# Layer 0's opening in two halves of the rows, with its modulation as dot products along the free axis and five latent blocks feature by feature

## The chip, the cores and the metric

The kernel runs on one core of a Trainium2 chip. The metric is the device time of one execution in microseconds (us), with the median of several runs. The engines are TensorE (PE), VectorE (DVE), ScalarE (ACT) and GpSimd (POOL); SP issues nearly all of the DMAs, in the order of its own queue.

## The reference, cut to what matters

A transformer of two layers over 1024 tokens of 1024 features, batch 1, float32. Each layer normalises its rows, modulates them by a vector computed from `c`, and projects them. Layer 0 has eight latent (MLA) heads and eight stick-breaking heads, layer 1 differential heads.

```python
c_act = jax.nn.silu(c)
for i in range(DEPTH):
    mod = c_act @ ada_w[i] + ada_b[i]
    shift, scale, gate = jnp.split(mod, 3, axis=-1)
    h = rms_norm(x, norm_g[i]) * (1.0 + scale[:, None, :]) + shift[:, None, :]
    ...
proj = h @ w_in
cuts = np.cumsum([MLA_Q_LORA, MLA_KV_LORA, MLA_ROPE, SB_W, SB_W, SB_W]).tolist()
cq, ckv, kr, q_sb, k_sb, v_sb, z = jnp.split(proj, cuts, axis=-1)
q = (rms_norm(cq, q_norm_g) @ w_uq).reshape(B, S, MLA_HEADS, MLA_NOPE + MLA_ROPE)
kv = (rms_norm(ckv, kv_norm_g) @ w_ukv).reshape(B, S, MLA_HEADS, MLA_NOPE + MLA_V)
```

`cq` has 384 columns and `ckv` 256: five blocks of 128 columns, called the latent blocks here (numbers 16 to 20 of the weights).

## The kernel before, in words

Float32 products run on TensorE as three passes over parts rounded to 12 bits: `split` (L155) takes hi on ScalarE (L159) and lo = src - hi on VectorE or GpSimd (L154), and `mm3` (L172) is hi x hi, hi x lo, lo x hi. `wprep` (L164) loads the weights of a block of 128 columns (512 KB) into `w_st`, a staging tile of a pool with two buffers, and splits them. The features of the normalised rows lie on the partitions: `hT[k]` holds features 128 k and on of all 1024 tokens, hi and lo.

The opening (L500 to L706) works under one pool, `a0`. All eight tiles of x are loaded and their squares summed, on ScalarE (L526) and VectorE (L523) in turn; `rstd_cols` (L188) makes 1/rms by thirteen small VectorE instructions; the rows are scaled in place (L532, L534). `ada_block(k)` (L538) then computes shift and scale of 128 features: `ada_st`, 1 MB of weights with the input feature on the partitions, is multiplied by `c_act` and accumulated by eight VectorE instructions of 128x256 (L542, L544) into `ack`, whose partitions TensorE sums with a matrix of ones (L547); four transposes of each half of the tokens follow (L554), and `modulate` (L237) scales and shifts them on ScalarE into `hf` and splits them, the lo part on GpSimd for blocks 1 to 6.

The first three latent blocks run feature by feature: while block k of `hT` is made, the 18 matmuls of block k - 1 run into six PSUM banks. Blocks 19 and 20 follow one after the other through `latent` (L611) and `dense_fm` (L177). The latents' evacuations store hi and lo parts to DRAM; `behind` is the last store of the first three. The modulation of layer 1 and both gates come from `ada_rest` (L589): two sets n = 0, 1 of eight loads of 1 MB each and 64 VectorE sweeps of 128x512 (L478, L480) into `acc`, and column sums of `acc` on TensorE (L487). It is a generator, stepped by `more(n)`, and every step is placed after `ready` (the last block of `hT`) and `behind`. Then come the rotated shared key `krt` (L642, 48 matmuls), the row factors `te` and `to` (L681 to L686), and four z blocks (L700), each two halves of 24 matmuls through a bank of a pool of three (`s_bank`), evacuated by ScalarE (L249) and a VectorE product (L251). The first head's projection, `qk_dense` into banks called `psd`, opens the attention.

The order within each engine is set when the kernel is built: a scheduler lays the instructions of the program out engine by engine and interleaves what is written in sequence, `tc.issue_after(x)` holds what is written inside it behind x, and a tile of a pool waits for the last reader of the buffer that it takes over.

Of the kernel before, what the change touches and what calls it, by code (L numbers as in the profile page):

```python
# [72 lines left out]
def kernel(ctx, tc, a, out):  # L73
# [33 lines left out]
    # scratch in DRAM  # L107
# [19 lines left out]
    # constants  # L127
# [49 lines left out]
    def dense_fm(w, rhs, evac, bank=None):  # L177
        """feature-major rows of one block of 128 columns, in two halves of the tokens"""
# [9 lines left out]
    def rstd_cols(pool, ss, n, scale, eps, name, extra=None, bufs=2):  # L188
        """(scale * ss + eps * extra) ** -0.5 of [P, n] columns"""
# [16 lines left out]
    def row_out(pool, cols, n, dst, bank):  # L206
        """[P, n] columns (query in block, block) to rows of n blocks in DRAM"""
# [22 lines left out]
    def row_sums(tile_of, nt, bank):  # L230
        """sums over the partitions of tile_of(t), as columns [P, nt]"""
# [14 lines left out]
    def z_evac(z, func, scale):  # L246
        """z * sigmoid(z), or twice that from tanh(z / 2)"""
# [16 lines left out]
    def v_rows(vs, hi, lo, n):  # L264
        """token-major halves of the values in vs; hi(g), lo(g) of four token tiles"""
# [13 lines left out]
    def pieces(i):  # L279
        """(first key, keys, computed keys) of the banks of query block i"""  # L280
# [5 lines left out]
    def scores(i, pairs, mask):  # L286
        """pairs of (stationary, moving) summed into the scores of query block i, one bank a piece"""
# [12 lines left out]
    def transpose_chunk(c, pa, pb):  # L300
        """[q, k] weights of query blocks 2c, 2c+1 to tiles [k, (kb 2j+1 | kb 2j), 256 q]"""
# [18 lines left out]
    def pv_chunk(dst, tiles, passes):  # L320
        """dst[dv, 256] = sum over key blocks; passes(kb) -> [(stationary, 0 hi | 1 lo)]"""
# [39 lines left out]
    def qk_dense(w, hT, b_t, bank=None):  # L361
        """[qh;qh], [ql;0], [kh;kl] of one head whose weights are [q | k]"""
# [21 lines left out]
    def par_view(ap, par, seq=False):  # L384
        """the tokens of chunks par and 2 + par; with seq of chunks 2 par and 2 par + 1"""
# [26 lines left out]
    def finish_half(pool, pv, par, e, ot, seq=False):  # L412
        """add the two halves ([vh|vl] or [vl|vh]) of a bank holding the chunks of par_view"""
# [7 lines left out]
    def load_wo(layer, half, f2s, alloc, gate, eng):  # L421
        """feature blocks 2 f2, 2 f2 + 1 of one half of the columns, times the gate, split"""
# [34 lines left out]
    def out_half(ys, wo, fs, x_, xr, bank):  # L457
        """x_ = xr + rows of y times columns of wo"""
# [11 lines left out]
    def ada_sweep(pool, src, acc):  # L470
        """acc[p, n] = sum over kk of c[128 kk + p] ada_w[128 kk + p, n] for 2048 columns"""
# [11 lines left out]
    def ada_cols(dst, bias, acc):  # L483
        """sums over the partitions of the 2048 columns of acc, as [P, 16], and the bias"""
# [9 lines left out]
    X_TAGS = [("lsq0", 1), ("lsq1", 1), ("lsq2", 1), ("zb", 2), ("zb", 2), ("lat_h", 2), ("lat_h", 2), ("lat_l", 2)]  # L494

    # =====================================================================
    # layer 0: modulation, transposed rows, latents
    # =====================================================================
    hT = [(res(f"h0h{k}"), res(f"h0l{k}")) for k in range(KC)]
    with tc.tile_pool(name="a0", bufs=1, reuse_waits="tile") as a0:  # L500
        sgc = a0.tile([P, 8], F32, name="sgc")
        nc.scalar.activation(sgc, c_sb, AF.Sigmoid)
        nc.vector.tensor_mul(c_act, c_sb, sgc)
        ada_st = {}

        def ada_load(k):
            ada_st[k] = a0.tile([P, KC, 256], F32, name="ada_st", tag="ld", bufs=NLD)
            dma(ada_st[k].rearrange("p r c -> p (r c)"), a["ada_k"][k])
            return ada_st[k]

        # normalised rows
        xts = []
        junka = a0.tile([P, 2, D], F32, name="junka", tag="acc")
        for g in range(2):
            ss = a0.tile([P, 4], F32, name="ss", tag="ss", bufs=2)
            for j in range(4):
                t = 4 * g + j
                tag, bufs = X_TAGS[t]
                xt = a0.tile([P, D], F32, name="xt", tag=tag, bufs=bufs)
                dma(xt, a["x"][t * P:t * P + P, :])  # L520
                if j % 2:
                    junk = a0.tile([P, D], F32, name="junk", tag="junk")
                    nc.vector.tensor_tensor_reduce(junk, xt, xt, op0=ALU.mult, op1=ALU.add, scale=1.0, scalar=0.0,  # L523
                                                   accum_out=ss[:, j:j + 1])
                else:
                    nc.scalar.activation(junka[:, 0, :], xt, AF.Square, accum_out=ss[:, j:j + 1])  # L526
                xts.append(xt)
            rs = rstd_cols(a0, ss, 4, 1.0 / D, 1e-6, "rc")
            for j in range(4):
                xt = xts[4 * g + j]  # L530
                if SC[4 * g + j] == "a":
                    nc.scalar.activation(xt, xt, AF.Copy, scale=rs[:, j:j + 1])  # L532
                else:
                    nc.vector.tensor_scalar(xt, xt, rs[:, j:j + 1], None, op0=ALU.mult)  # L534
            if g == 0:
                ada_load(0)

        def ada_block(k):  # L538
            """modulation of features 128 k and on, applied to their transposed rows"""
            st = ada_st[k] if k in ada_st else ada_load(k)  # L540
# [7 lines left out]
            nc.vector.tensor_tensor(modc[0][:, k::8], ps[:, 0:2], adab[:, k:16:8], op=ALU.add)  # L548
            nc.vector.scalar_tensor_tensor(gsc[0][:, k:k + 1], modc[0][:, 8 + k:9 + k], 1.0, ng[:, k:k + 1],
                                           op0=ALU.add, op1=ALU.mult)  # L550
            for g in range(2):
                tr = t_bank()
                for j in range(4):
# [654 lines left out]
```

## Time and profile before

| | |
|---|---|
| runs | 1490.88, 1488.34, 1491.48 us, median 1490.88 |
| profiled execution: span on the profile | 1489.6 us |
| TensorE busy | 1394.9 us, 94% |
| VectorE busy | 956.8 us, 64% |
| ScalarE busy | 670.5 us, 45% |
| GpSimd busy | 446.2 us, 30% |
| DMA | 189.85 MB, mean 127 GB/s |

The page's busy times are unions over the whole span, so they hide in which stretch an engine is waited for. The timeline lists instructions of one engine by their start, merged where they follow each other in one form, with the idle time just before them and what ended it. The granted clock is TensorE's, 1.00 for the full 2.4 GHz.

### The profile page before, as it was taken

The page shows a single profiled execution, that of the slowest core. Times are in us where ns is not written, and L with a number is a line of the kernel's source. Part 1 is how long each engine was busy: PE and PEld are TensorE (multiplying, and loading weights), DVE is VectorE, ACT ScalarE, POOL GpSimd, SP SyncE. Part 2 cuts the span into 40 slices and gives each one's busy share as a digit, 9 for nine tenths or more (in the row PEclk, how much of TensorE's full clock was granted, in tenths as well). Part 3 has the DMA queues.
Part 4 walks back from the last instruction along what each step waited for, and adds up shares of the span by engine and source line. Part 5 has one row for each costly group of instructions (what it writes and reads, how often), then busy time and mean ns, then how long its engine had stood idle before and what let it go on. Part 6 is the DMA issues. An engine that isn't in the chain of part 4 may idle for free.

```text
span 1489.6 us, 20993 instructions
## 1 busy us (share of the span) xinstructions
PE 1394.9 (94%) x7328; PEld 1160.7 (78%) x7328; DVE 956.8 (64%) x2155; ACT 670.5 (45%) x1368; POOL 446.2 (30%) x509
## 2 busy tenths in 40 slices
PE   3899999999998899999879899999999999997797
PEld 2777888888886688887767688888888888886686
DVE  7769637667779865576557526665565756567674
ACT  4452145555556653555345324444444535354321
POOL 1534221132427354635133321133121222134100
PEclk9999999999999999999989999999999999999899
DMA  9269522131224166433747131324232324346262
GB/s 375 67 261 382 206 77 75 49 90 50 75 69 186 36 188 213 136 123 100 215 136 268 29 108 48 86 85 114 71 100 64 92 64 114 78 111 179 82 201 93
DMA packets 109640, 189.85 MB, mean 127 GB/s; under 512 B 8736, under 2 KB 70040, under 8 KB 107488
## 3 DMA queue, kind: packets, MB, share of 16 engines
q1 hardware_dynamic: 109536, 188.53, 39.9%
q8 instruction: 58, 0.95, 0.3%
q14 instruction: 46, 0.38, 0.1%
HBM read 131.23 MB, written 39.27 MB: 114 GB/s over the span
## 4 chain that ended last, share of the span: by engine, by line
PE 40%; DVE 5%; DMA 4%; issue 1%; POOL 1%; ACT 1%; SPq 0%; DVEq 0%; ACTq 0%; POOLq 0%
PE psd L173 8%; PE psd L175 8%; PE psd L174 8%; PE sc L294 4%; PE pv L328 3%; PE sc L173 2%; PE sc L174 2%; PE sc L175 2%; DMA y_hi<-yh_d 1%; DMA w_st<-in_wo_dram 1%; PE pv L234 1%; PE tr L308 1%; PE tr L309 1%; PE tr L310 1%; DVE g L1029 1%
## 5 line engine op out<-in xcount | busy, mean ns | idle before, releaser
L154 POOL TENSOR_TENSOR w_lo<-w_st,w_hi 128x1024 fp32r<-128x1024 f32 (+2 forms) x63 | 153.6, 2440 | 370.7 <-ACT w_hi L159 370.4
L154 DVE TENSOR_TENSOR pt_l<-tr,pt_h 128x512 fp32r<-128x512 f32 (+1 forms) x240 | 148.8, 630 | 104.9 <-ACT pt_h L159 97.4
L159 ACT CAST pt_h<-tr 128x512 fp32r<-128x512 f32 (+1 forms) x240 | 126.2, 547 | 147.0 <-PE tr L310 136.1
L175 PE MATMUL psd<-h1h,w_lo 128*128 128x512 f32 x448 | 177.0, 395 | 0.0
L174 PE MATMUL psd<-h1l,w_hi 128*128 128x512 f32 x448 | 176.2, 393 | 0.0
L173 PE MATMUL psd<-h1h,w_hi 128*128 128x512 f32 x448 | 176.1, 393 | 0.0
L294 PE MATMUL sc<-qk_k,qk_a 128*128 128x512 f32 (+2 forms) x288 | 104.8, 369 | 3.6 <-ACT g L747 1.3
L173 PE MATMUL psd<-h0h,w_hi 128*128 128x512 f32 x264 | 106.7, 404 | 0.0
L174 PE MATMUL psd<-h0l,w_hi 128*128 128x512 f32 x264 | 105.6, 400 | 0.0
L175 PE MATMUL psd<-h0h,w_lo 128*128 128x512 f32 x264 | 105.2, 398 | 0.0
L294 PE MATMUL sc<-qk_k,qk_b 128*128 128x512 f32 (+2 forms) x288 | 98.5, 349 | 0.0
L1029 DVE CUSTOM_DVE_ANT_0 g<-sc,tz 128x512 f32<-128x512 f32 (+3 forms) x128 | 72.1, 585 | 40.1 <-PE sc L294 33.7
L159 ACT CAST w_hi<-w_st 128x1024 fp32r<-128x1024 f32 x56 | 58.9, 1052 | 86.4 <-PE sc L174 36.2
L174 PEld LDWEIGHTS psd<-h1l,w_hi 128*128 128x128 f32 x448 | 84.2, 188 | 17.1
L175 PEld LDWEIGHTS psd<-h1h,w_lo 128*128 128x128 f32 x448 | 84.2, 188 | 16.1
L173 PEld LDWEIGHTS psd<-h1h,w_hi 128*128 128x128 f32 x448 | 84.2, 188 | 16.1
L328 PE MATMUL pv<-pt_l,vt 128*128 128x256 f32 x320 | 88.7, 303 | 8.2 <-DVE pt_l L154 7.4
L1035 ACT ACTIVATE g<-g,st 128x640 f32<-128x640 f32 (+3 forms) x64 | 63.4, 990 | 67.8 <-DVE st L1034 63.1
L328 PE MATMUL pv<-pt_h,vt 128*128 128x256 f32 x320 | 89.5, 296 | 3.3 <-POOL pt_h L314 1.7
L749 DVE TENSOR_TENSOR_SCAN g<-g 128x640 f32<-128x640 f32 (+3 forms) x32 | 68.7, 2148 | 14.7 <-ACT g L746 14.6
L328 PEld LDWEIGHTS pv<-pt_l,vt 128*128 128x128 f32 x320 | 62.0, 194 | 12.0 <-issue 4.7
L328 PEld LDWEIGHTS pv<-pt_h,vt 128*128 128x128 f32 x320 | 61.8, 193 | 9.5 <-DVE ot L418 2.7
(469 smaller groups left out, 3743.3 us busy)
## 6 DMA issues: line engine op xcount, KB each, us to landing
w_st<-in_w_dram SPq DMA_DIRECT2D x46, 512.0 KB
ada_st<-in_ada_k_dram SPq DMA_DIRECT2D x8, 1024.0 KB
ada_st<-in_ada_w_dram SPq DMA_DIRECT2D x16, 512.0 KB
ada_st<-in_ada_w_dram SPq DMA_DIRECT2D x8, 1024.0 KB
w_st<-in_wo_dram SPq DMA_DIRECT2D x16, 512.0 KB
yh_d<-yh SPq DMA_DIRECT2D x28, 256.0 KB
yl_d<-yl SPq DMA_DIRECT2D x28, 256.0 KB
w_st<-in_wv_dram SPq DMA_DIRECT2D x12, 512.0 KB
```

Source lines behind the costliest of these rows:

```text
L154: return (nc.vector if eng == "vec" else nc.gpsimd).tensor_tensor(out_, x_, y_, op=ALU.subtract)
L159: nc.scalar.copy(hi, src)
L173: mm(ps, sh, mh, start=start, stop=False)
L174: mm(ps, sh, ml, start=False, stop=False)
L175: mm(ps, sl, mh, start=False, stop=stop)
L234: mm(ps[:, t:t + 1], tile_of(t), ones, start=True, stop=True)
L294: mm(ps[:, :nn], st[:, q], mv[:, lo_:lo_ + nn], start=m == 0, stop=not diag and m == len(pairs) - 1)
L308: nc.tensor.transpose(tr[:, P:256], pb[:, (2 * j + 1) * P:(2 * j + 2) * P], identf)
L328: mm(dst, st, tt[w][:, m * 256:m * 256 + 256], start=j == 0 and m == 0 and x == 0, stop=j == n - 1 and m == 1 and x == len(ps_) - 1)
L749: nc.vector.tensor_tensor_scan(ur, ur, ur, 1.0, op0=ALU.mult, op1=ALU.bypass)
L1029: nc.vector.tensor_tensor_reduce(e_[:, sl], ps, tz[:, S - L + sl.start:S - L + sl.stop], op0=ALU.add, op1=ALU.max, scale=1.0, scalar=-3e38 ...
L1035: nc.scalar.activation(e_[:, :L], e_[:, :L], AF.Exp, scale=0.125, bias=st[:, 2 + c:3 + c], accum_out=lst[:, c1:c1 + 1] if c == 0 else st[: ...
```

## The change

Everything lies in the opening of layer 0.

- `ada_k` becomes `ada_t`: the same 1 MB a block with the output feature on the partitions and the input features along the free axis. `c` is loaded to all partitions as `cb` (512 KB) and passed through the sigmoid there. The modulation of a block is two dot products on VectorE over 1024 elements (the form of L523); `ack` and its sums on TensorE are gone.
- x comes in two halves of four tiles. All squares are on ScalarE; of four scalings three are on ScalarE. The second half is loaded behind `ada_load(3)` and normalised behind block 3's modulation.
- The lo parts of `hT` are all on VectorE. The lo parts of the five latent weights are on VectorE for the first three, on GpSimd for the last two.
- Five latent blocks run feature by feature on the first 512 tokens (three `s_bank`, two `d_bank`; 15 matmuls a block of features), then the second 512 tokens block by block (24 matmuls each).
- `behind` is now the last store of all five. The rotary table, lambda and the relative-position rows stand behind the latents.

```diff
+        cb = a0.tile([P, D], F32, name="cb", tag="cs")
+        dma(cb, a["c"].to_broadcast([P, D]))
+        csg = a0.tile([P, D], F32, name="csg", tag="junkd")
+        nc.scalar.activation(csg, cb, AF.Sigmoid)
+        nc.vector.tensor_mul(cb, cb, csg)
...
         def ada_block(k):
-            ac = a0.tile([P, 256], F32, name="ack", tag="ack", bufs=2)
-            nc.vector.tensor_scalar(ac, st[:, 0, :], c_act[:, 0:1], None, op0=ALU.mult)
-            for r in range(1, KC):
-                nc.vector.scalar_tensor_tensor(ac, st[:, r, :], c_act[:, r:r + 1], ac, op0=ALU.mult, op1=ALU.add)
-            ps = t_bank()
+            m = a0.tile([P, 2], F32, name="adm", tag="adm", bufs=2)
             for n in range(2):
-                mm(ps[:, n:n + 1], ac[:, n * P:n * P + P], ones, start=True, stop=True)
+                nc.vector.tensor_tensor_reduce(junk, ada_st[k][:, n, :], cb, op0=ALU.mult, op1=ALU.add, scale=1.0, scalar=0.0,
+                                               accum_out=m[:, n:n + 1])
...
+        x0 = x_load(0)
+        ada_load(0)
+        normed = x_norm(x0)
+        with tc.issue_after(normed.ins):
+            known = ada_block(0)
+            x_mod(0, 0, x0, "vec")
+            with tc.issue_after(known.ins):
+                for b in range(3):
+                    w_load(b)
+                ada_load(1)
+                for b in (3, 4):
+                    w_load(b)
+        ada_load(2)
+        loaded = ada_load(3)
+        with tc.issue_after(loaded.ins):
+            x1 = x_load(1)
+        fb = [s_bank(), s_bank(), s_bank(), d_bank(), d_bank()]
+        for k in range(KC):
+            if k + 1 < KC:
+                known = ada_block(k + 1)
+                _, done = x_mod(0, k + 1, x0, "vec")
+                if k + 4 < KC:
+                    ada_load(k + 4)
+            if k == 2:
+                with tc.issue_after(known.ins), tc.issue_after(done.ins):
+                    x_norm(x1)
+            for b in range(5):
+                mm3(fb[b], wl[b][0][:, k, :], wl[b][1][:, k, :], hT[k][0][:, :512], hT[k][1][:, :512], k == 0, k == KC - 1)
...
+        for k in range(KC):
+            ready, _ = x_mod(1, k, x1, "vec")
+        for b in range(5):
+            latent_evac(b, 0, fb[b])
+        for b in range(5):
+            ps = (s_bank, d_bank)[b % 2]()
+            for k in range(KC):
+                mm3(ps, wl[b][0][:, k, :], wl[b][1][:, k, :], hT[k][0][:, 512:], hT[k][1][:, 512:], k == 0, k == KC - 1)
+            behind = latent_evac(b, 1, ps)
```

How the instructions now stand, at three places (helper lines are one lower in the changed kernel; names in brackets are the semaphores that an instruction waits for, DMAHW those of earlier DMAs).

SP's queue in the opening, the kernel before, from the second weight load on:

```order
L80 DMA w_st<-in_w_dram 128x1024 [waits DMAHW3_49]
L80 DMA ada_st<-in_ada_k_dram 128x2048 [waits DMAHW4_49]
L80 DMA ada_st<-in_ada_k_dram 128x2048 [waits DMAHW5_49]
L80 DMA ada_st<-in_ada_k_dram 128x2048 [waits DMAHW6_49]
L80 DMA ada_st<-in_ada_k_dram 128x2048 [waits DMAHW7_49]
L80 DMA ada_st<-in_ada_k_dram 128x2048 [waits DMAHW0_49]
L80 DMA tab<-in_tab_dram 32x8 [waits DMAHW1_49]
L80 DMA pos_i<-in_pos_dram 128x1 [waits DMAHW2_49]
L80 DMA ada_st<-in_ada_k_dram 128x2048 [waits DMAHW3_49,DVE_49]
```

and the changed kernel, from the first weight load on:

```order
L79 DMA w_st<-in_w_dram 128x1024
L79 DMA w_st<-in_w_dram 128x1024 [waits DMAHW0_49]
L79 DMA ada_st<-in_ada_t_dram 128x2048 [waits DMAHW1_49]
L79 DMA pos_i<-in_pos_dram 128x1 [waits DMAHW2_49]
L79 DMA tab<-in_tab_dram 32x8 [waits DMAHW3_49]
L79 DMA w_st<-in_w_dram 128x1024 [waits DMAHW7_49,DMAHW4_49,DVE_49]
L79 DMA w_st<-in_w_dram 128x1024 [waits DMAHW5_49,DMAHW0_49,DVE_49]
L79 DMA w_st<-in_w_dram 128x1024 [waits DMAHW6_49,DMAHW4_49,DVE_49]
L79 DMA ada_st<-in_ada_t_dram 128x2048 x2
```

Before, five `ada_st` loads follow the two weight loads, with no wait for an engine ahead of them. Now three weight loads that wait for VectorE stand ahead of `ada_st` 2 and 3.

VectorE where the gate's column sums (`gt`) are read, the kernel before:

```order
L488 TENSOR_TENSOR gt<-tr,smalls 128x16
L478 TENSOR_SCALAR acc<-ada_st,c_act 128x512 x4
L480 SCALAR_TENSOR_TENSOR acc<-ada_st,c_act,acc 128x512 x4
L211 COPY row<-pv 8x128
L480 SCALAR_TENSOR_TENSOR acc<-ada_st,c_act,acc 128x512 x4
L251 TENSOR_TENSOR zb<-zb,sc 128x512
L480 SCALAR_TENSOR_TENSOR acc<-ada_st,c_act,acc 128x512
L211 COPY row<-tr 16x128
L480 SCALAR_TENSOR_TENSOR acc<-ada_st,c_act,acc 128x512 x3
L251 TENSOR_TENSOR zb<-zb,sc 128x512
```

and the changed kernel:

```order
L487 TENSOR_TENSOR gt<-tr,smalls 128x16
L477 TENSOR_SCALAR acc<-ada_st,c_act 128x512 x4
L479 SCALAR_TENSOR_TENSOR acc<-ada_st,c_act,acc 128x512 x8
L210 COPY row<-tr 16x128
L712 COPY te<-rqb 64x1024
L713 TENSOR_TENSOR te<-rqb,cs 64x1024
L716 TENSOR_TENSOR to<-rqb,cs 64x1024
L717 COPY to<-rqb 64x1024
L479 SCALAR_TENSOR_TENSOR acc<-ada_st,c_act,acc 128x512 x2
L250 TENSOR_TENSOR zb<-zb,sc 128x512 x2
```

`zb` is the product that evacuates a bank of a z block. Behind `gt` one product follows after twelve sweeps before; now the first two products stand behind twelve sweeps, `te`, `to` and two more sweeps, and they are those of the first z block.

TensorE at the first column sums of `acc`, the changed kernel, where four of the sixteen stand between the halves of the first z block:

```order
L172 MATMUL sc<-h0h_141,w_hi 128x512
L173 MATMUL sc<-h0l_142,w_hi 128x512
L174 MATMUL sc<-h0h_141,w_lo 128x512
L486 MATMUL tr<-ones_sq,acc 128x1 x4
L172 MATMUL sc<-h0h_127,w_hi 128x512
L173 MATMUL sc<-h0l_128,w_hi 128x512
L174 MATMUL sc<-h0h_127,w_lo 128x512
```

and at the others, where twelve stand between the first and the second z block:

```order
L174 MATMUL sc<-h0h_141,w_lo 128x512
L208 MATMUL pv<-identf,rlr 8x128
L486 MATMUL tr<-ones_sq,acc 128x1 x12
L172 MATMUL sc<-h0h_127,w_hi 128x512
L173 MATMUL sc<-h0l_128,w_hi 128x512
L174 MATMUL sc<-h0h_127,w_lo 128x512
```

and the kernel before, where all sixteen stand in the second z block:

```order
L173 MATMUL sc<-h0h_133,w_hi 128x512
L174 MATMUL sc<-h0l_134,w_hi 128x512
L175 MATMUL sc<-h0h_133,w_lo 128x512
L487 MATMUL tr<-ones_sq,acc 128x1 x16
L173 MATMUL sc<-h0h_135,w_hi 128x512
L174 MATMUL sc<-h0l_136,w_hi 128x512
L175 MATMUL sc<-h0h_135,w_lo 128x512
```

The sums of set n = 0 moved ahead by one half to one z block, and were divided.

## Rows read from the trace of the kernel before

**Rows 1.** The page, first part: engine, busy us, share of the span, instructions.

```profile
PE 1394.9 (94%) x7328; PEld 1160.7 (78%) x7328; DVE 956.8 (64%) x2155; ACT 670.5 (45%) x1368; POOL 446.2 (30%) x509
```

**Rows 2.** Windows: stretch, length, busy us by engine, granted clock, DMA share, GB/s.

```profile
20.00:30.00 10.00, 5.38 (x16) 3.22 (x16) 9.79 (x22) 3.95 (x6) 3.13 (x1) 1.00 1.01 418
30.00:40.00 10.00, 8.78 (x41) 6.23 (x40) 9.81 (x24) 4.25 (x7) 2.95 (x3) 1.00 0.85 337
40.00:50.00 10.00, 5.46 (x20) 4.39 (x19) 9.79 (x17) 3.80 (x6) 5.19 (x4) 0.69 0.23 67
52.00:179.00 127.00, 125.38 (x597) 101.85 (x596) 96.39 (x165) 44.02 (x63) 44.27 (x20) 0.96 0.63 245
```

**Rows 3.** Timeline of TensorE: start, us, line, operation, [idle before <-releaser].

```profile
25.18 0.80 PE L173 MATMUL sc<-h0h,w_hi 128*128 128x512 f32 x1 [4.00 <-ACT h0h L159]
...
38.72 0.40 PE L174 MATMUL sc<-h0l,w_hi 128*128 128x512 f32 x1
...
38.95 0.40 PE L175 MATMUL sc<-h0h,w_lo 128*128 128x512 f32 x1
...
45.88 0.98 PE L547 MATMUL tr<-ones_sq,ack 128*128 128x1 f32 x4 [4.54 <-DVE ack L544]
```

**Rows 4.** Timeline of TensorE, column sums and first head.

```profile
138.96 3.82 PE L487 MATMUL tr<-ones_sq,acc 128*128 128x1 f32 x32
...
179.23 0.63 PE L173 MATMUL psd<-h0h,w_hi 128*128 128x512 f32 x1
...
179.66 0.63 PE L174 MATMUL psd<-h0l,w_hi 128*128 128x512 f32 x1
...
183.07 0.63 PE L173 MATMUL psd<-h0h,w_hi 128*128 128x512 f32 x1
```

**Rows 5.** Timeline of VectorE in the opening.

```profile
15.93 1.22 DVE L523 CUSTOM_DVE_ANT_0 junk<-xt 128x1024 f32<-128x1024 f32 x1
...
17.07 0.08 DVE L523 DVE_READ_ACCUMULATOR2_ANT ss<- 128x1 f32 x1
...
17.07 0.48 DVE L544 SCALAR_TENSOR_TENSOR ack<-ada_st,c_act,ack 128x256 f32<-128x256 f32 x1
...
38.02 9.14 DVE L544 SCALAR_TENSOR_TENSOR ack<-ada_st,c_act,ack 128x256 f32<-128x256 f32 x9
```

**Rows 6.** Timeline of GpSimd beside it.

```profile
39.70 2.87 POOL L154 TENSOR_TENSOR h0l<-hf,h0h 128x512 fp32r<-128x512 f32 x2 [0.37 <-ACT h0h L159]
42.54 2.52 POOL L154 TENSOR_TENSOR w<-w_st,w 128x1024 fp32r<-128x1024 f32 x1
```

**Rows 7.** Timeline of ScalarE in the opening.

```profile
5.17 1.06 ACT L526 ACTIVATE junka<-xt 128x1024 f32<-128x1024 f32 x1 [2.34 <-DMA xt<-in_x_dram]
...
14.27 2.19 ACT L532 ACTIVATE xt<-xt,rcr 128x1024 f32<-128x1024 f32 x2 [0.29 <-DVE rcr L203]
...
19.06 1.04 ACT L159 CAST w_hi<-w_st 128x1024 fp32r<-128x1024 f32 x1 [0.19 <-DMA w_st<-in_w_dram]
...
23.70 0.78 ACT L239 ACTIVATE hf<-tr,modc,gsc 128x512 f32<-128x512 f32 x1 [3.59 <-DVE gsc L549]
...
24.50 0.62 ACT L159 CAST h0h<-hf 128x512 fp32r<-128x512 f32 x1
```

**Rows 8.** Timeline of SP's queue: DMA issues.

```profile
9.00 6.66 SPq L80 DMA_DIRECT2D ada_st<-in_ada_k_dram  x5
...
93.65 6.22 SPq L80 DMA_DIRECT2D ada_st<-in_ada_w_dram  x7
```

**Rows 9.** Chain of waits near the end of the program: start, us, what.

```profile
1338.69 4.63 DMA w_st<-in_wo_dram
```

**Rows 10.** Timeline of VectorE: sweeps, `te` and `to`, a z product.

```profile
165.86 6.53 DVE L480 SCALAR_TENSOR_TENSOR acc<-ada_st,c_act,acc 128x512 f32<-128x512 f32 x8
...
172.32 0.67 DVE L681 COPY te<-rqb 64x1024 f32<-64x1024 f32 x1
...
176.21 0.69 DVE L251 TENSOR_TENSOR zb<-zb,sc 128x512 f32<-128x512 f32 x1
```

More of the change, by code (lines that the diff above doesn't have):

```diff
@@ L509, in ada_load @@
[L509 to L514, printed above, removed]
-            ss = a0.tile([P, 4], F32, name="ss", tag="ss", bufs=2)
[L516 to L527, printed above, removed]
+            ada_st[k] = a0.tile([P, 2, D], F32, name="ada_st", tag="ld", bufs=NLD)
@@ new lines, in ada_load, with wide, x_load, x_norm @@
+            return dma(ada_st[k].rearrange("p i d -> p (i d)"), a["ada_t"][k])
+        def wide(name, tag):
+            return a0.tile([P, S], F32, name=name, tag=tag, bufs=4)
+        def x_load(g):
+            ts = []
+            for t in range(4 * g, 4 * g + 4):
+                xt = wide("xt", "ab"[g])
+                dma(xt, a["x"][t * P:t * P + P, :])
+                ts.append(xt)
+            return ts
+        def x_norm(xts):
+            ss = a0.tile([P, 4], F32, name="ss", tag="ss", bufs=2)
+            for j, xt in enumerate(xts):
+                junk = a0.tile([P, D], F32, name="junk", tag="junk")
+                nc.scalar.activation(junk, xt, AF.Square, accum_out=ss[:, j:j + 1])
@@ L548, in ada_block @@
[L548 to L553, printed above, removed]
-                    nc.tensor.transpose(tr[:, j * P:(j + 1) * P], xts[4 * g + j][:, k * P:(k + 1) * P], identf)
-                last = modulate(a0, hT, 0, k, slice(g * 512, g * 512 + 512), tr, "act", "vec" if LOK(k, g) else "pool")
@@ L556, in ada_block @@
-            return last
-        ada_block(0)
-        wq3 = [wprep(a["w0"][16 + b], eng_lo=WLO[b]) for b in range(2)]
-        w3 = a0.tile([P, 2, 1024], F32R, name="w3", tag="acc")
-        wq3.append(wprep(a["w0"][18], alloc=lambda name: w3[:, 0 if name == "w_hi" else 1, :]))
-        first = [[s_bank(), s_bank()], [s_bank(), d_bank()], [d_bank(), v_bank()]]
+            m = a0.tile([P, 2], F32, name="adm", tag="adm", bufs=2)
+            for n in range(2):
+                junk = a0.tile([P, D], F32, name="junkd", tag="junkd")
+                nc.vector.tensor_tensor_reduce(junk, ada_st[k][:, n, :], cb, op0=ALU.mult, op1=ALU.add, scale=1.0, scalar=0.0,
+                                               accum_out=m[:, n:n + 1])
@@ new lines, in ada_block, with x_mod @@
+            nc.vector.tensor_tensor(modc[0][:, k::8], m, adab[:, k:16:8], op=ALU.add)
+            return nc.vector.scalar_tensor_tensor(gsc[0][:, k:k + 1], modc[0][:, 8 + k:9 + k], 1.0, ng[:, k:k + 1],
+                                                  op0=ALU.add, op1=ALU.mult)
+        def x_mod(g, k, xts, lo):
+            tr = t_bank()
+            for j in range(4):
+                nc.tensor.transpose(tr[:, j * P:(j + 1) * P], xts[j][:, k * P:(k + 1) * P], identf)
+            hf = a0.tile([P, 512], F32, name="hf", tag="hf", bufs=3)
+            sl = slice(g * 512, g * 512 + 512)
+            nc.scalar.activation(hf, tr, AF.Identity, scale=gsc[0][:, k:k + 1], bias=modc[0][:, k:k + 1])
+            hi = nc.scalar.copy(hT[k][0][:, sl], hf)
+            return sub(lo, hT[k][1][:, sl], hf, hT[k][0][:, sl].bitcast(F32)), hi
@@ new lines, with w_load @@
+        in_a0 = lambda tag, bufs: (lambda t_: (lambda name: t_[:, 0 if name == "w_hi" else 1, :]))(
+            a0.tile([P, 2, 1024], F32R, name="wl", tag=tag, bufs=bufs))
+        wl = []
+        def w_load(b):
+            alloc = None if b < 2 else in_a0("acc", 1) if b == 2 else in_a0("ld", NLD)
+            wl.append(tuple(t_.rearrange("p (k c) -> p k c", c=P)
+                            for t_ in wprep(a["w0"][16 + b], eng_lo=WLO[b], alloc=alloc)))
+        x0 = x_load(0)
+        ada_load(0)
@@ L564 @@
         for k in range(KC):
             if k + 1 < KC:
-                ready = ada_block(k + 1)
-            for b in range(3):
-                wh, wl = (t.rearrange("p (k c) -> p k c", c=P) for t in wq3[b])
-                for half in range(2):
-                    sl = slice(half * 512, half * 512 + 512)
-                    mm3(first[b][half], wh[:, k, :], wl[:, k, :], hT[k][0][:, sl], hT[k][1][:, sl], k == 0, k == KC - 1)
-        w4 = a0.tile([P, 2, 1024], F32R, name="w4", tag="ld", bufs=NLD)
@@ L635, in latent, with latent_norm @@
+        def latent_norm(b0, n, row_d):
+            part = lambda half, b: sqt[half, b // 2][:, b % 2 * 512:b % 2 * 512 + 512]
+            for half in range(2):
+                for b in range(b0 + 1, b0 + n):
+                    nc.gpsimd.tensor_tensor(part(half, b0), part(half, b0), part(half, b), op=ALU.add)
+            ss = row_sums(lambda t: part(t // 4, b0)[:, t % 4 * P:t % 4 * P + P], NT, v_bank)
+            r = rstd_cols(a0, ss, NT, 1.0 / (n * P), 1e-6, "rl")
             row_out(a0, r, NT, row_d, v_bank)
-            return stored
```

130 lines of the change are left out of this document (57 added, 73 removed).

## The prediction

> **What bounds the kernel now.** I first read the page's busy times: TensorE is busy 94% of the span [rows 1], so nearly all of the 1489.6 us is its own work, and a change that leaves the matmuls as they are can only touch the idle rest. Then the windows of 10 us over the opening, which show where that rest lies: TensorE works 5.38, 8.78 and 5.46 us of the three windows from 20 to 50 us, VectorE about 9.8 of 10 in each, and the DMA share falls from 1.01 to 0.23 once the loads are in [rows 2]. So the opening waits for VectorE, not for memory. TensorE's timeline says for what: the first latent matmul starts at 25.18, and at 45.88 it has waited 4.54 us for `ack`, the sum over features of one block [rows 3]. That wait also costs clock: the granted clock of 40 to 50 us is 0.69 [rows 2], and the matmuls behind the wait stand at 0.63 us a row instead of 0.40, at the 1.2 GHz level; they follow each other every 0.43 us there [rows 4] against 0.23 [rows 3]. VectorE's rows show why `ack` is late: nine instructions of 128x256 took 9.14 us [rows 5] while GpSimd ran subtractions of 2.87 and 2.52 us [rows 6]. From 52 us to the first matmul of the first head, at 179.23 [rows 4], it is busy for 125.4 of 127 us [rows 2]. That start, 179.23, is what I forecast anew: from there on the order of every engine is the same in both kernels.
>
> **The change, part by part.** The profiled span is 1489.6 us, 1.3 under the median of the three runs, 1490.88; differences worked out against the span are put on the median. What a measurement of this kernel can tell from no change is about 0.2%, or 3 us.
>
> *Modulation.* Eight instructions of 128x256 a block (at best 0.48 each) and a column sum on TensorE become two dot products over 1024 elements. The form stands in the trace: 1.22 us and 0.08 for its result [rows 5]; two make 2.4 to 2.6 us, about a half microsecond less than eight short ones, and the round trip over TensorE goes. That is a small gain a block; the column sums that go, 32 rows of the trace, were TensorE work of some 0.1 us each (32 others took 3.82 us [rows 4]), about 3 us in all.
>
> *Subtractions of the first half move from GpSimd to VectorE.* Each costs VectorE about 0.7 us (1.22 for twice the size [rows 5]), and the blocking of 2.5 to 2.9 us that GpSimd's cost it goes. Only the weights of the last two latent blocks stay on GpSimd; I charge 2 x 2.5 us to VectorE's chain.
>
> *First matmul.* The rows of x land from 5.17 us on [rows 7], and one load of `cb` (512 KB, 1.3 us at the 418 GB/s of [rows 2]) goes ahead of them. All squares of the half are on ScalarE; the scalings start as before at about 14.3, three of 1.1 us and one on VectorE end at 17.5 [rows 7]; the dot products of block 0 run beside them until 17.4. Two weight casts of 1.04, then 0.78 and 0.62 for the first transposed half block [rows 7] give a first matmul at 21.0, 4.2 us earlier than 25.18.
>
> *Starvation behind it.* Five latent blocks want five weight loads, but the staging pool has two buffers. The third, fourth and fifth wait on SP for VectorE's subtractions, and `ada_st` of blocks 2 and on, with x's second half, stand behind them in SP's order. In the kernel before, SP had issued `ada_st` 1 to 5 between 9.00 and 15.66 [rows 8]. Now: subtraction of weights 0 ends at 19.75, the third load goes out at 19.8. It is alone in the queue; a load of this size, waited for alone, took 4.63 us in the chain of waits [rows 9]; I take 4.0, the bounds are 2.5 (its bytes at 418 GB/s twice over) and 5.5. It lands at 23.8, cast 1.04 and subtraction 1.22 end at 26.1, the fifth load goes out, and `ada_st` 2 behind it. With 0.5 and 1 MB ahead (1.3 and 2.5 us) and the same landing time it is there at 32.6. Its dot products end at 35.0, its h at 36.9. Until then TensorE has blocks 0 and 1 alone, 30 matmuls, at the low clock 13 us of the 16. So most of the lead is gone by 37.
>
> The Trainium skill, page "DMA: Bandwidth & Descriptors", section on the anatomy of one DMA, gives each transfer a fixed cost of about 2 us besides bytes over 436 GB/s, which speaks against serial loads as here. By it the lone load would be an estimated 3.2 us instead of 4.0, and `ada_st` 2 about 0.8 us earlier; row 4.63 is above either.
>
> *Rest of the first half.* `ada_st` 3 lands at 35.1, x's second half at 40.2 and `ada_st` 4 at 42.8 (2.5 us a MB). Four squares on ScalarE end at 45.2, and VectorE, in order, waits for them ahead of block 4, whose h comes at 48.6; then 52.7, 57.9 and 62.0, some 4 to 5 us a block of VectorE (dot products 2.5, subtraction 0.7, the second half's scaling, GpSimd's blocking) against 15 x 0.23 plus transposes, 4.0 us, on TensorE. The first half ends at 66, the second, 120 matmuls at 0.23 and small waits, at **97**, which I call L. I give it 93 to 101.
>
> *Behind the latents.* Here two waits appear that the kernel before has not, because the sweeps for layer 1 (64 instructions over 16 MB) are released by the last latent store in both: at 93.65 before [rows 8], 45 us ahead of the column sums at 138.96 [rows 4], and now at L + 2.2 = 99, with four of these sums only 72 matmuls behind the latents. TensorE reaches them at L + 21.5 (72 x 0.227 = 16.3, row sums and table rows 4, small gaps). The 29th sweep that they need: first load lands at L + 6.5, 2.5 us a MB, the eighth at L + 24, its sweep of 0.8 (eight took 6.53 [rows 10]) with others in between at about L + 27. **Wait 1: 6 us** (bounds 3 and 9). Then four sums 1.0, 24 matmuls 5.6, twelve sums and a transpose 3.2: L + 37.3. The next is 24 matmuls of the second z block, 5.6, with 2.4 for the clock (after the sums of the kernel before the first matmuls of the head still stand at 0.63 us [rows 4]). Its other half needs the bank that VectorE's product of the first z block frees, and that stands on VectorE behind the twelve sums (`gt`), twelve sweeps, the four instructions of `te` and `to`, 172.32 to 176.21 or 3.9 us [rows 10], and two sweeps: 14 x 0.65 + 3.9 + 0.2 = 13.2, to L + 50.5. **Wait 2: 5.2 us** (bounds 2 and 8). From there 72 matmuls 16.8, clock 2.4, sixteen sums 3.9 (recorded as 32 rows, 3.82 [rows 4]), 48 matmuls 11.2, clock 2.7: 37.0. The head starts at L + 87.5 = 184.5. The kernel before starts it at 179.23 at the low clock; the ten slow rows there, to 183.07, cost 10 x 0.2 = 2 us, which the new kernel has paid already. So **184.5 - 179.2 - 2 = 3.3 us slower**. Median 1490.9 + 3.3 = 1494.2. TensorE's removed 3 us, its earlier start and the lost waits of the old opening are in L.
>
> **The rivals.** *A, TensorE sets the first half (not slower).* If the lone load takes near 2.5 us and GpSimd blocks nothing, `ada_st` 2 is there at 29 and each block takes TensorE's 4.0 instead of VectorE's 4 to 5. Then 21.0 + 8 x 4 + 28 + 7 for the slow start gives L = 88 to 89, the head at 176, 8 earlier than in my sum: 1486. For it: dot products of 1.22 are the trace's own figure, and the 9.14 goes. Against it: one SP queue in order, and two staging buffers. It decides when `ada_st` 2 lands before 30.
>
> *B, the two waits are hidden.* If the sums find their sweeps done, 11.2 us go from 184.5: 173.3, or 1483. For it: TensorE hardly waits at the same sums before. Against it: the release at L + 2 and 2.5 us a MB are hard to beat. If only one wait shows, it is 5 to 6 less, 1488 to 1489: no change.
>
> *C, starvation deeper.* x's second half and `ada_st` 4 to 7 late by the two GpSimd subtractions and a 5.5 us load each: L = 101 to 103, and 1499 to 1501.
>
> *D, no net effect.* L = 94, both waits there: 1491. That the dot products don't run as meant is no case: their form is in the trace.
>
> **How the numbers follow.** Forecast (L 95 to 99, both waits; 1492 to 1497) 0.42; A 0.2; B with one or two waits hidden 0.13; C 0.1; D 0.15. Below 1488 lie A and half of B: faster 0.28. Within 3 us lie D, the other half of B and the low end of the forecast: same 0.28. Slower 0.44. Leaving out the end of B and that of C, the range is 1484.5 to 1500; the forecast's own is 1492 to 1497. The time is that of the forecast, **1494.2**.
>
> **What would show it.** Right: first latent matmul near 21; `ada_st` 2 issued near 26 behind the weight loads; a hole or slow clock on TensorE at 30 to 37; latents ending near 97; a wait of 3 to 9 us before the four sums on `acc`, and one of 2 to 8 on `zb` in the second z block; the head at 182 to 187. Wrong: the blocks following each other at 4 us from 21 on (A), no idle before the sums (B), or a difference that arises behind the head's start.

## The result: 0.54% slower

| | kernel before | changed kernel |
|---|---|---|
| median of the runs made side by side | 1489.61 us (4 runs) | 1498.72 us (4 runs, 1497.78 to 1501.4) |
| span of the profiled execution | 1489.6 us | 1496.0 us |
| first v transposes of the first head | 203.13 us | 209.98 us |

The ratio is 1.0054, with a 95% interval of 1.0029 to 1.008: 8 us slower, 4 to 12. Up to the first v transposes of the first head (`tr<-identf,vs`), a place behind everything that the change moves, the changed kernel has lost 6.85 us; from there to the end it takes 1286.0 us and the kernel before 1286.5. So the loss lies ahead of the heads, and these transposes serve as the mark below.

It doesn't lie in the opening. The last matmul of the latents ends at 108.95 in the kernel before and at 96.76 in the changed one, 12.2 us earlier. From there to the mark the kernel before takes 94.2 us and the changed one 113.2; TensorE stands idle for 1.6 us of the one stretch and for 14.0 of the other. About 3 us of work, the relative-position rows and some row sums, comes ahead of this point before and behind it now. The last matmul of the latents, the kernel before:

```profile
108.56 0.39 PE L175 MATMUL sc<-h0h,w_lo 128*128 128x512 f32 x1
```

and the changed kernel:

```profile
96.36 0.40 PE L174 MATMUL sc<-h0h,wl 128*128 128x512 f32 x1
```

TensorE's busy time on the page is as it was [rows 1], so over the whole span what was added is idle time.

```profile
PE 1395.0 (93%) x7296; PEld 1158.9 (77%) x7296; DVE 935.1 (63%) x2127; ACT 678.8 (45%) x1380; POOL 438.5 (29%) x498
```

The waits of TensorE from 60 to 180 us name two that the kernel before doesn't have. Columns: what TensorE was to run, what it waited for, us in total, times, the longest.

```profile
PE tr L486 <- DVE acc L479: 7.8, 1, 7.8
PE sc L172 <- DVE zb L250: 6.1, 1, 6.1
```

TensorE's timeline around them, against [rows 4]: the first sums come at 126.38 after a wait of 7.83; the matmuls behind them stand at 0.63 us a row until 132.07, with a granted clock of 0.50 from 128 to 132 us, the 1.2 GHz level, and the second wait ends at 152.04. The head starts at 188.22, at the full clock, where the kernel before started at 179.23 and paid some 2 us for the low one.

```profile
126.38 1.84 PE L486 MATMUL tr<-ones_sq,acc 128*128 128x1 f32 x8 [7.83 <-DVE acc L479]
...
128.66 0.63 PE L173 MATMUL sc<-h0l,w_hi 128*128 128x512 f32 x1
...
132.07 0.60 PE L172 MATMUL sc<-h0h,w_hi 128*128 128x512 f32 x1
...
135.84 2.74 PE L486 MATMUL tr<-ones_sq,acc 128*128 128x1 f32 x24
...
152.04 0.80 PE L172 MATMUL sc<-h0h,w_hi 128*128 128x512 f32 x1 [6.13 <-DVE zb L250]
...
188.22 0.39 PE L172 MATMUL psd<-h0h,w_hi 128*128 128x512 f32 x1
```

In TensorE's order the first four sums stand 36 matmuls earlier than before and the other twelve 12 earlier; a z block has 48, so that is three quarters and one quarter of a block, and not one half to one block as the section on the change has it.

VectorE's timeline shows why TensorE waits. The last sweep that the first sums need runs at 125.50. `gt` follows the last sums at 138.62, and the product that frees a bank for the second z block comes at 151.30, behind twelve sweeps, `te`, `to` and two more.

```profile
125.50 0.73 DVE L479 SCALAR_TENSOR_TENSOR acc<-ada_st,c_act,acc 128x512 f32<-128x512 f32 x1
...
138.62 0.17 DVE L487 TENSOR_TENSOR gt<-tr,smalls 128x16 f32<-128x16 f32 x1 [2.29 <-PE tr L486]
138.71 1.95 DVE L477 TENSOR_SCALAR acc<-ada_st,c_act 128x512 f32<-128x512 f32 x4
140.58 5.38 DVE L479 SCALAR_TENSOR_TENSOR acc<-ada_st,c_act,acc 128x512 f32<-128x512 f32 x8
...
146.08 0.67 DVE L712 COPY te<-rqb 64x1024 f32<-64x1024 f32 x1
...
149.25 0.69 DVE L717 COPY to<-rqb 64x1024 f32<-64x1024 f32 x1
...
151.30 1.28 DVE L250 TENSOR_TENSOR zb<-zb,sc 128x512 f32<-128x512 f32 x2
```

From 20 to 50 us the opening is only a little better than before, and starved as well. The windows against [rows 2]: TensorE works 8.08 us of the window from 20 to 30 (5.38 before), 6.99 from 30 to 40 (8.78 before) and 8.31 from 40 to 50 (5.46 before).

```profile
20.00:30.00 10.00, 8.08 (x22) 4.40 (x22) 6.90 (x11) 4.44 (x6) 2.39 (x1) 1.00 0.63 204
30.00:40.00 10.00, 6.99 (x25) 5.21 (x26) 7.21 (x14) 2.74 (x4) 2.39 (x1) 0.85 1.01 416
40.00:50.00 10.00, 8.31 (x39) 6.36 (x38) 6.16 (x19) 7.01 (x12) 0.00 (x0) 0.98 1.02 423
```

SP issued three weight loads over 6.27 us, each behind a wait for VectorE; `ada_st` 2 and 3 followed at 26.41, and x's second half.

```profile
20.08 6.27 SPq L79 DMA_DIRECT2D w_st<-in_w_dram  x3
26.41 0.90 SPq L79 DMA_DIRECT2D ada_st<-in_ada_t_dram  x2
27.35 1.99 SPq L79 DMA_DIRECT2D xt<-in_x_dram  x4
```

VectorE, busy for 9.8 us of each ten here before [rows 2], waits 2.23 us for `ada_st` 2 and 1.76 for `ada_st` 4.

```profile
32.53 2.13 DVE L543 CUSTOM_DVE_ANT_0 junkd<-ada_st,cb 128x1024 f32<-128x1024 f32 x1 [2.23 <-DMA ada_st<-in_ada_t_dram]
...
43.62 1.23 DVE L543 CUSTOM_DVE_ANT_0 junkd<-ada_st,cb 128x1024 f32<-128x1024 f32 x1 [1.76 <-DMA ada_st<-in_ada_t_dram]
```

TensorE starts at 21.24, 3.9 us earlier than in [rows 3], and waits for the third block of features at 37.25.

```profile
21.24 1.20 PE L172 MATMUL sc<-h0h,w_hi 128*128 128x512 f32 x2
...
37.25 1.11 PE L553 MATMUL tr<-identf,xt 128*128 128x128 f32 x4 [2.43 <-ACT hf L556]
```

### The profile page after: what moved, and what is told of

Its sections match the earlier page's. It is cut to its first block, busy times and chain, and to the rows that moved or that the text cites. A ratio compares the mean times of both kernels' runs of the same rounds, so it can differ in the third digit from the quotient of the medians.

```text
span 1496.0 us, 20920 instructions
## 1 busy us (share of the span) xinstructions
PE 1395.0 (93%) x7296; PEld 1158.9 (77%) x7296; DVE 935.1 (63%) x2127; ACT 678.8 (45%) x1380; POOL 438.5 (29%) x498
## 4 chain that ended last, share of the span: by engine, by line
PE 39%; DMA 6%; DVE 4%; issue 2%; POOL 1%; ACT 1%; SPq 0%; DVEq 0%; ACTq 0%; POOLq 0%
PE psd L172 8%; PE psd L173 8%; PE psd L174 8%; PE sc L293 4%; PE pv L327 3%; PE sc L172 2%; PE sc L173 2%; PE sc L174 2%; DMA w_st<-in_wo_dram 1%; PE pv L233 1%; DMA xp_d<-xr 1%; PE tr L307 1%; PE tr L308 1%; PE tr L309 1%; DMA tz<-rel_d 1%
## 5 line engine op out<-in xcount | busy, mean ns | idle before, releaser
L153 POOL TENSOR_TENSOR w_lo<-w_st,w_hi 128x1024 fp32r<-128x1024 f32 (+2 forms) x61 | 162.5, 2665 | 356.4 <-ACT w_hi L158 356.1
```

The source lines that it names most:

```text
L153: return (nc.vector if eng == "vec" else nc.gpsimd).tensor_tensor(out_, x_, y_, op=ALU.subtract)
```

## The experiments

Theory W: the two waits and the low clock behind them are the loss. Theory S: one SP queue in order starves the first half. Rivals: the opening itself cost the time (O); VectorE has too much to do between the latents and the head, in whatever order (V). The median of the kernel before was 1488.8 to 1490.0 beside these runs.

| kernel | latents end | v transposes | median | ratio to before, 95% interval |
|---|---|---|---|---|
| before | 109.0 | 203.1 | | |
| changed | 96.8 | 210.0 | 1498.7 | 1.0054 (1.0029 to 1.008) |
| 1 early release | 96.3 | 207.9 | 1498.7 | 1.0057 (1.004 to 1.0073) |
| 2 three loads first | 96.3 | 208.3 | 1497.1 | 1.0051 (1.0032 to 1.0071) |
| 3 both | 96.4 | 206.3 | 1496.3 | 1.0053 (1.003 to 1.0075) |
| 4 before, dot products alone | 106.4 | 198.1 | 1492.4 | 1.0021 (1.0 to 1.0042) |
| 5 sweeps held | 96.1 | 202.7 | 1491.3 | 1.0024 (1.001 to 1.0037) |
| 6 early and held | 96.1 | 201.8 | 1488.1 | 0.9992 (0.9973 to 1.0011) |
| 7 five loads first | 93.1 | 204.8 | 1495.7 | 1.0059 (1.0038 to 1.008) |
| 8 queue, early, held | 92.9 | 196.9 | 1484.8 | 0.9982 (0.9964 to 1.0) |
| 9 held, `te` and `to` late | 96.6 | 195.6 | 1485.0 | 0.9971 (0.9953 to 0.999) |
| 10 queue, early, held, late | 93.0 | 189.9 | 1479.7 of seven; an eighth execution took 2737.6 | 0.9931 (0.9908 to 0.9954) |
| 11 as 10, weights on VectorE | 91.7 | 191.8 | 1479.5 | 0.9944 (0.9922 to 0.9967) |
| 12 as 4, profiled again | 106.8 | 198.4 | 1488.3 | 0.9988 (0.9972 to 1.0004) |

The latents end with the last matmul on `wl`, in the kernel before and in 4 and 12 with that on the weights of block 20; times in the first two columns are of the profiled execution. Medians of a few runs lie up to 9 us off their own profiled execution (kernel 4: 1492.4 beside 1483.2), so the mark tells the stretch and the ratio the kernel. Kernels 1 to 4, 5 to 8 and 9 to 12 ran on three chips, each group beside the kernel before, so between the groups ratios compare and medians don't.

**1. Sweeps released early.**

```diff
-            latent_evac(b, 0, fb[b])
+            behind = latent_evac(b, 0, fb[b])
...
-            behind = latent_evac(b, 1, ps)
+            latent_evac(b, 1, ps)
```

> Sweeps released by the last store of the first half of the latents (near 75 us) instead of the last store of all (near 100). Theory W (the loss is the two waits behind the column sums of acc, 7.8 and 6.1 us, and the low clock behind the first): no idle of over 1 us before the first sums, the latents end at 97 to 98 as in the changed kernel, the head starts at 174 to 180 instead of 188.2, median 1485 to 1491. Rival O (the opening itself cost the time, and a wait at the sums only changes its place): the head starts at 186 to 188, median 1497 to 1500.

The first sums found their sweeps done, without a wait, and yet the head started at 186.13 and the time did not move. In place of both waits there is one of 12.18 us for `krt`, the product of the shared key:

```profile
PE sc L172 <- DVE krt L705: 12.2, 1, 12.2
```

VectorE's timeline: the earlier sweeps bring `gt` forward in its order, and 24 sweeps of the second set with it, from 124.27 to 140.79; they now stand ahead of `krt`.

```profile
124.18 0.17 DVE L487 TENSOR_TENSOR gt<-tr,smalls 128x16 f32<-128x16 f32 x1 [1.19 <-PE tr L486]
...
126.05 5.37 DVE L479 SCALAR_TENSOR_TENSOR acc<-ada_st,c_act,acc 128x512 f32<-128x512 f32 x8
...
138.07 2.07 DVE L479 SCALAR_TENSOR_TENSOR acc<-ada_st,c_act,acc 128x512 f32<-128x512 f32 x3
...
140.79 1.28 DVE L705 TENSOR_TENSOR krt<-sc,cs 128x512 f32<-128x512 f32 x2
```

So the lateness of the release is not the cause by itself, and W fell in that form. O's numbers came out, but its reason wasn't shown: the opening ends 12 us ahead of the kernel before, and the wait is new. What was left to try is the order on VectorE.

**2. Three `ada_st` loads and x's second half ahead of the waiting weight loads.**

```diff
-                for b in range(3):
+                for b in range(2):
                     w_load(b)
                 ada_load(1)
-                for b in (3, 4):
+                ada_load(2)
+                loaded = ada_load(3)
+                for b in (2, 3, 4):
                     w_load(b)
-        ada_load(2)
-        loaded = ada_load(3)
```

> Loads of ada_st 2 and 3 and of the second half of x stand on SP ahead of the three weight loads that wait. Theory S (one queue in order starves the first half): ada_st 2 lands near 17 instead of 32.5, no TensorE wait for hf near 37, the latents end at 88 to 92 instead of 97.6, both waits at the sums stay at 5 to 9 us since the sweeps move with the latents, median 1490 to 1493. Rival (the weights of blocks 18 to 20, now behind 4 MB more, set the first half): the latents end at 95 to 98, median 1496 to 1499.

The rival came out in the number: the latents end at 96.3, and the median is 1497.1. Block 2's first dot product moved from 32.53 to 24.06, but block 4's did not, 43.61 beside 43.62, and for another reason than in the changed kernel. It waits for no load: it stands on VectorE behind the norm of x's second half, which waits 3.00 us for the squares on ScalarE and ends with the scaling at 42.95.

```profile
24.06 1.22 DVE L543 CUSTOM_DVE_ANT_0 junkd<-ada_st,cb 128x1024 f32<-128x1024 f32 x1
...
38.34 0.24 DVE L191 TENSOR_SCALAR rch<-ss 128x4 f32<-128x4 f32 x1 [3.00 <-ACT junk L529]
...
42.95 0.75 DVE L535 TENSOR_SCALAR xt<-xt,rcr 128x1024 f32<-128x1024 f32 x1
43.61 1.22 DVE L543 CUSTOM_DVE_ANT_0 junkd<-ada_st,cb 128x1024 f32<-128x1024 f32 x1
```

SP's queue was late as well. The three weight loads now take from 20.89 to 35.71, since the fifth waits for a subtraction at 34.12, and `ada_st` 4 to 7 stand behind it:

```profile
20.89 14.82 SPq L79 DMA_DIRECT2D w_st<-in_w_dram  x3
35.76 1.92 SPq L79 DMA_DIRECT2D ada_st<-in_ada_t_dram  x4
```

So both the queue and VectorE's order stood in the way of block 4. S wasn't settled by this run, and a later one moved these loads too.

**3. Edits 1 and 2 together.**

> Both edits. Theory W and S together: the two gains add, the latents end at 88 to 92 and the head starts at 165 to 172, median 1477 to 1484. If the sweeps (2.5 us a MB of loads, 64 instructions) then bound the stretch to the head by themselves: no earlier than in the better of the two alone, 1485 to 1491.

Neither: the head started at 184.5, better than either alone (186.1, 186.6) by about 2 us, with a wait of 10.1 us for `rlr`, the norm of the second latent, whose small instructions stand among the same sweeps. The median, 1496.3, is above both forecasts.

**4 and 12. The kernel before with the dot products alone.** `ada_block`, `cb` and the layout of the weights as in the changed kernel, all else as before.

> The kernel before with the dot products alone (transposed weights, c on all partitions); tokens not in halves, three latent blocks feature by feature, order of loads as before. If the dot products are the good part of the change: no wait for ack (4.5 us before) and no column sums, latent blocks 8 to 10 us earlier, the sums of acc still without a wait, median 1481 to 1485. If the opening before was bound by something else (its 16 subtractions, loads of weights): the head within 3 us of 179, median 1488 to 1492.

> The kernel with the dot products alone, profiled a second time, since its first profile showed the v transposes 5.0 us earlier than before while the median of its runs was above. If its opening takes several courses: transposes 3 us or more later than 198.1 in this profile. If it is steady: 198.1 within 1 us, and the median, 1488 to 1493, differs behind the opening.

The mark came at 198.1 and 198.4 in two profiles, 4.7 to 5.0 us earlier than before, so the gain up to there is steady. The sums of `acc` are without a wait, as forecast, but the latents end only 2.2 to 2.5 us earlier, where 8 to 10 were forecast, and the median of kernel 4, 1492.4, is above the 1481 to 1485 of that forecast. The times don't show the gain: 1.0021 and 0.9988, on opposite sides of one. In the two profiled executions it is not lost behind the mark, where they take 1283.3 and 1287.2 us to the end and the kernel before 1286.5; what the dot products alone bring to the time stays open.

**5. Each step of the sweeps that is written behind a product of `krt` or of a z block is held behind that product on VectorE.**

```diff
-            with tc.issue_after(ready.ins), tc.issue_after(behind.ins):
+            with ExitStack() as es:
+                for g in [ready, behind] + gate[-1:]:
+                    es.enter_context(tc.issue_after(g.ins))
...
-            nc.vector.tensor_mul(krt[:, sl], ps, cs[:, sl])
+            gate.append(nc.vector.tensor_mul(krt[:, sl], ps, cs[:, sl]))
```

and the same for the z products.

> The changed kernel, with each step of the sweeps that is written behind a product of krt or of a z block held behind that product on VectorE; released by the last latent store as before. Theory W (what costs is where krt, the z products and the sums stand in VectorE's order against the sweeps): no TensorE idle of over 2 us for acc, krt or zb, the head starts at 162 to 168 instead of 188.2 with the second set of sums (about 6 us with its clock) inside it, median 1481 to 1487. Rival V (VectorE has too much to do between the latents and the head, in whatever order): a wait of 8 us or more shows at another place, the head and its sums no earlier than 184, median 1495 to 1499.

Between the two: the wait for the sums is gone, without an earlier release, the mark comes 7.3 us earlier than in the changed kernel, and the ratio is 1.0024 instead of 1.0054. The head, at 174.1, and the median, 1491.3, lie between W's numbers and V's. The holding changed TensorE's order too: the first sums stand behind 144 matmuls of `krt` and the z blocks instead of 72 and start at 147.0 instead of 126.4, and so find their sweeps done. One wait of 8.97 us for `zb` is left. VectorE's timeline: sixteen sweeps, then `te`, which waits 3.33 us for `rqb` from DRAM, and the z products of the first block behind `to`.

```profile
118.24 1.27 DVE L708 TENSOR_TENSOR krt<-sc,cs 128x512 f32<-128x512 f32 x2
119.44 10.67 DVE L479 SCALAR_TENSOR_TENSOR acc<-ada_st,c_act,acc 128x512 f32<-128x512 f32 x16
133.43 1.72 DVE L715 COPY te<-rqb 64x1024 f32<-64x1024 f32 x1 [3.33 <-DMA rqb<-rq_d]
...
136.42 1.22 DVE L719 TENSOR_TENSOR to<-rqb,cs 64x1024 f32<-64x1024 f32 x1
137.65 0.69 DVE L720 COPY to<-rqb 64x1024 f32<-64x1024 f32 x1
138.37 1.28 DVE L739 TENSOR_TENSOR zb<-zb,sc 128x512 f32<-128x512 f32 x2
```

**6. The same with the early release.**

> The same holding, and the sweeps released by the last store of the latents' first half. Theory W: as with the late release or up to 2 us better, median 1480 to 1486, since the holding and not the release decides. If the late release costs by itself: 3 us or more better than the late one. Rival V: 1495 to 1498.

The wait for `zb` is 4.06 us here, and the mark 1 us earlier. The holding brought the most; what the release adds, 0.9992 against 1.0024, is at the edge of the two intervals. The median, 1488.1, is above W's 1480 to 1486.

**7. Five `ada_st` loads and x's second half ahead of the third or fifth weight load.** As in 2, with `ada_load(4)` and `ada_load(5)` written between `w_load(3)` and `w_load(4)`.

> Loads of ada_st 2 to 5 and of x's second half stand ahead of the third or fifth weight load, sweeps as in the changed kernel. Theory S (a weight load that waits on SP holds back the next ada_st): ada_st 4 lands before 36 instead of 43.6, the latents end at 89 to 93 and the median falls to 1490 to 1494, with both waits at the sums kept. Rival (VectorE's and ScalarE's work on x's second half sets the end of the first half): the latents end at 95 to 98, 1496 to 1499.

SP issued `ada_st` 4 and 5 at 24.64, and block 4's first dot product came at 35.30:

```profile
20.91 2.83 SPq L79 DMA_DIRECT2D w_st<-in_w_dram  x2
24.64 1.60 SPq L79 DMA_DIRECT2D ada_st<-in_ada_t_dram  x2
35.41 3.72 SPq L79 DMA_DIRECT2D w_st<-in_w_dram  x2
```

```profile
35.30 1.22 DVE L543 CUSTOM_DVE_ANT_0 junkd<-ada_st,cb 128x1024 f32<-128x1024 f32 x1
```

The latents end at 93.1, 3.7 us sooner, and the mark comes 5.2 us sooner; both waits stay (6.85 and 6.92 us). The stretch moves as S has it, at the upper end of what it forecast. But the product now also stands ahead of the norm of x's second half in VectorE's order, where it stood behind it in 2, and no run tells what either did alone. The time doesn't show the gain: the ratio is 1.0059, and the median, 1495.7, lies above S's range and just below the rival's.

**8. Edits 7, 1 and 5 together.**

> Queue order, early release and holding together. W and S together: latents end at 89 to 93, the head starts at 155 to 162, median 1474 to 1481, faster than the kernel before. W alone: as with the holding alone, 1480 to 1486.

Latents at 92.9, the mark at 196.9, and 0.9982: as fast as the kernel before or faster. S and W had forecast a time lower by almost 4 us or more; the median, 1484.8, is in the range of W alone, although the mark comes 4.9 us earlier than in kernel 6. The wait for `zb` is again there with 4.17 us, behind `te` and `to`, which took 8.1 us instead of 3.9.

**9. The changed kernel with the holding, and `te` and `to` written behind the last z product.** Opening and release are those of the changed kernel.

> The changed kernel with its opening and release as they are, the steps of the sweeps held behind krt and the z products, and te and to written behind the last z product. Theory W (the waits behind the latents are the whole loss): no TensorE idle of over 2 us for acc, krt or zb, the first v transposes of the first head at 192 to 196 (before 203.1, changed 210.0), median 1480 to 1484. Rival V: the time shows as another wait of over 5 us and the transposes come at 201 or later, median 1489 to 1492.

The waits of TensorE from 60 to 180 us are now small:

```profile
PE tr L486 <- DVE acc L479: 2.1, 2, 1.7
PE sc L172 <- DVE zb L731: 1.3, 1, 1.3
```

On TensorE the first sums now stand behind 174 matmuls of `krt` and the z blocks instead of 72:

```profile
143.01 3.76 PE L486 MATMUL tr<-ones_sq,acc 128*128 128x1 f32 x32
```

The mark is at 195.6, 14.3 us earlier than in the changed kernel and 7.5 earlier than before, and the kernel is faster than before, 0.9971, with a median 1 us above what W forecast. With its opening untouched, the order behind the latents alone takes it from slower to faster: this is what decides between W and O, and V, which had the mark at 201 or later, falls with it. It is the order on two engines, though: the products ahead of the sweeps on VectorE, and the sums further back on TensorE.

**10 and 11. The same with the queue order and the early release; then also the lo parts of all latent weights on VectorE.**

> The same with the queue order and the early release: latents end near 94, no wait of over 2 us behind them, v transposes at 188 to 193, median 1476 to 1481. If what is left behind the latents is VectorE's own work: transposes at 194 to 197 as with te and to in front, median 1483 to 1486.

> The same with the lo parts of the last two latent weights on VectorE as well: VectorE stood idle near 36 to 43 there, so the weights come 1 to 2 us sooner, v transposes 1 to 2 us earlier than in the one before, median the same within 2 us. If VectorE is what sets the first half: 2 us or more later.

Kernel 10 came as W and S have it, with waits of 1.4 and 1.3 us, and is the best of the study together with 11, 0.7% and 0.6% faster than before:

```profile
PE tr L486 <- DVE acc L479: 1.4, 1, 1.4
PE sc L172 <- DVE zb L734: 1.3, 1, 1.3
```

In 11 the latents end 1.3 us sooner as expected, but the mark comes 1.9 us later; the two intervals overlap, and the difference is left open.

## Why the prediction was right, and where its size was off

*Side and mechanism.* It forecast slower, with both waits by name and place; the time, 1498.7, is in the range of 1484.5 to 1500, but above the forecast's own 1492 to 1497, and the ratio's interval, 4 to 12 us, begins just above the 3.3 us forecast. It lies close to the 1499 of rival C, but not by C's mechanism: L was 96.8 and not 101 to 103.

*The opening* came as worked out. First matmul 21.24 (21.0), `ada_st` 2 issued at 26.41 (26.1), its dot product at 32.53 (32.6), latents' end 96.8 (97). The 4.0 us for a load waited for alone came as 3.6, issue at 20.08 and cast at 23.70, against the 4.63 of [rows 9]. By the fixed cost that the Trainium skill gives (page "DMA: Bandwidth & Descriptors", section on the anatomy of one DMA) the estimate was 3.2 us; the section fits it to transfers issued on GpSimd's path, and this load, issued by SP, lies between 3.2 and 4.0.

*Wait 1* was sized 6 us and took 7.83: TensorE arrived at 118.55, as worked out (L + 21.5), but the 29th sweep ended at 126.2 instead of 124. The sweeps began at 104.66, when the first load was there, where the sum had 103.5. Behind the one at 108.88 none waited for a load: they followed each other in VectorE's own time, with small instructions of the latents' norms between pairs of 1.40 us, so four took about 2.8 us against the 2.5 us a MB of the sum.

*The term left out* is the clock behind wait 1: ten matmuls at 0.63 us, 2.0 us, where I charged the low clock behind the twelve sums, behind wait 2 and behind the sixteen sums, but not here. With the 1.8 us of wait 1 these 2.0 make the 3.7 us by which the head came late, 188.22 for 184.5; the other differences cancel.

*Wait 2* was sized 5.2 and took 6.13; from `gt` to the product were 12.7 us (13.2). The rest, 152.04 to 188.22, is 36.2 us (37.0).

*The rivals.* A needed `ada_st` 2 before 30: it came at 32.5. Experiments 2 and 7 bring its product to 24.1, and the latents end 0.5 and 3.7 us earlier, not the 8 of A. B had named the prize: with the waits hidden 173.3 for the head; experiment 9, which hides them, moves the mark 14.3 us. Its point against, the late release, holds only for sums that stay where they stand: in experiment 5 the wait for them goes with the release as late as it was, because they stand further back, and in experiment 1 an early release alone takes that wait away and brings nothing. What decides is the order behind the latents, of the products among the sweeps on VectorE and of the sums among the z blocks on TensorE; no run has the products ahead with the sums left in place, so the share of each is not shown. The prediction had the order, but read the sweeps' end as a matter of loads, 2.5 us a MB.

*Beyond the stretch* I took the time from the head on as equal. It is, 1286.0 and 1286.5 us in these two profiles, though such equality is not exact for other kernels (below).

## What to carry to other kernels

A gain in an opening is worth what the next in-order queue lets through: here 12.2 us at the end of the latents were eaten by work of low urgency, sweeps for the gates and layer 1, standing on VectorE ahead of the products that free a PSUM bank. When a stage is shortened, look at where the filler of the next stage stands in each engine's order, and hold it behind the products on the path; releasing filler earlier without that only moved the wait here (experiment 1). On a queue that issues in order, look also for loads that wait for a buffer ahead of loads that don't; to move them brought the latents 3.7 us forward in experiment 7, together with a change of VectorE's order.

## What the runs showed of the hardware that was not expected

With the same program behind the mark, the stretch from the mark to the end took between 1282.4 and 1291.8 us over fourteen profiles, the granted clock over the whole span lying between 0.969 and 0.979; single executions of one kernel spread over 10 us. Gains of some 5 us at the mark were seen in the profile and not in the median (kernels 4, 7).

Some VectorE instructions that ran beside a GpSimd subtraction or addition were stretched, of two inputs and also a copy of one. In kernel 8 a product of 64x1024 took 3.31 us and the copy behind it 2.79, where the product ahead of them took 1.22:

```profile
121.95 1.22 DVE L719 TENSOR_TENSOR te<-rqb,cs 64x1024 f32<-64x1024 f32 x1
123.20 3.31 DVE L722 TENSOR_TENSOR to<-rqb,cs 64x1024 f32<-64x1024 f32 x1
126.52 2.79 DVE L723 COPY to<-rqb 64x1024 f32<-64x1024 f32 x1
```

with GpSimd at work from 122.36 to 128.76:

```profile
122.36 3.07 POOL L731 TENSOR_TENSOR krt<-krt,krc 128x1024 f32<-128x1024 f32 x1 [9.97 <-ACT krc L730]
125.38 3.38 POOL L153 TENSOR_TENSOR w_lo<-w_st,w_hi 128x1024 fp32r<-128x1024 f32 x1
```

GpSimd was stretched as well: in the changed kernel its subtraction of 128x1024 that began at 112.29, while VectorE ran sweeps without a break until 126.2, took 16.16 us, and the one at 136.82 took 2.36.
